# Gate biases joined to the modulation's sums, and gate and context rows moved ahead, in a two-block transformer kernel on one core

## The chip, the cores and the metric

The program runs on one core of a Trainium2 chip. Its time is the time of one execution on the device, in microseconds. Before the change three runs took 1168.17, 1168.83 and 1171.95 us; the median is 1168.83.

## What is computed

Everything is float32 with 256 tokens of width 1024. The first block (two layers of retention, dilated attention and a gated unit, each with a feed-forward) yields the latents `x`. The second block has one even and one odd layer, and a second set of 256 tokens, the context. The change lies in the second block:

```python
# mod, mod_ctx: silu(c) @ w_mod + b_mod, silu(c_ctx) @ w_mod + b_mod  -> shift, scale, gate of each layer
h_lat = rmsnorm(x, g) * (1 + scale) + shift            # the context with its own shift and scale
h_ctx = rmsnorm(ctx, g) * (1 + scale_c) + shift_c
y_l, y_c = even_layer(h_lat, h_ctx, ...)               # Fourier mixing and latent attention, @ w_out
x   = x + gate * y_l
ctx = ctx + gate_c * y_c                               # read only by the odd layer's norm
x   = x + gate_2 * odd_layer(norm(x), norm(ctx), ...)  # windowed attention over latents and context
```

So each layer has three vectors, shift, scale and gate, for the latents and three for the context; the odd layer needs no gate for the context.

## The kernel before

**Weights and precision.** All weights stream through SBUF. Each piece of 128 rows (`raw`) is cut into a high part (`whi`, written by ScalarE) and a low part (`wlo`, by VectorE or GpSimd), and each product is made of three on TensorE: high by high, high by low, low by high. Activations are cut in the same way into `xh` and `xl`, after transposes into a bank called `tr`; there are two such banks.

**Order of the work.** One Python class, `Flow` (L126), keeps an account of when each operand is expected. Weight products form the backbone, and the steps of everything else are tasks (generators) which `Flow` puts between them when their operands should be there. What it decides is only the order on each engine: an instruction whose operand is late holds all that stands behind it on its engine.

**Modulation.** `mod_step` (L871) multiplies pieces of `w_mod` with the two condition vectors and adds the sums in `macc`; the first sum of a group is copied there (L886 on). For a gate, group `g % 3 == 2`, the finished sums, still without bias, go to a DRAM tile `gates` as rows (`gates<-macc`). They must be read back on all 128 partitions.

**Gate rows.** `gate_rows` (L1659) reads half a gate row, 512 columns, to all partitions (`gr<-gates`, 256 KB), reads the same half of the bias (`brow<-in_b_mod`, 256 KB), both on ScalarE's DMA queue, and adds them on GpSimd (`gr<-gr,brow`).

**The even layer** runs as two passes whose steps are interleaved: pass 0 for the context, pass 1 for the latents. A pass ends with the output projection `wo`: for each half `h` of the columns it calls `gate_rows` (L2067), and for each tile `t` of 128 tokens it makes 24 products in a bank `mm`, multiplies by the gate on VectorE (`wt<-mm,gr`) and adds the old row. In pass 1 the sum goes into `x` (GpSimd). In pass 0 (L2087 on) the old half row is read from DRAM (`cr<-in_ctx`), the sum is made on GpSimd (`cr<-cr,wt`) and written to DRAM (`cnew<-cr`).

**The context's second norm.** After pass 0's `wo`, `ctx_task` (L2094) reads each whole row tile back (`junk<-cnew`, 512 KB) and starts `modnorm_task` (L1038) on it: a sum of squares on ScalarE (`dump`), its power -1/2 on VectorE and GpSimd (`pe`, `rmod`), the row times that on ScalarE (`junk<-junk,rmod`), eight transposes, scale and shift of each block on VectorE (`junk<-tr,modA,modT`), and the split (`xh`, `xl`). The same task serves the latents after pass 1's `wo`.

**Attention in pass 1** runs beside pass 0's `wo`: exponentials `pe` on ScalarE with their sums `den`, reciprocals `rd`, the scaled weights `pe<-pe,rd` (one half on VectorE, one on GpSimd), their transposes `tr<-c,pe`, and the split `pp`. Queries come as `qn`, `qp` and `qr`.

**The odd layer** loads its constants and, late, its gate `ogl`, again with `gate_rows` (L2300 on). `nsink` is a small constant row that VectorE negates.

Of the kernel before, what the change touches and what calls it, by code (L numbers as in the profile page):

```python
# [38 lines left out]
# column ranges of the packed constants  # L39
# [9 lines left out]
def make_constants():  # L49
# [10 lines left out]
    # the retention's decay, gamma ** (q - k), as a factor of each key and one of each query  # L60
# [6 lines left out]
    # dilated branches: how many of the three hold a key, as a bias on unscaled scores  # L67
# [29 lines left out]
def two_pi_parts():  # L97
    from fractions import Fraction
    # 1 / (2 pi), cut in pieces of 12 bits
# [12 lines left out]
class Ev:  # L112
    """Something a step waits for: the time at which its data is expected."""
# [6 lines left out]
LAT = 0.22          # from one engine's result to another's start  # L120
# [5 lines left out]
class Flow:  # L126
    """The order in which TensorE's work is issued: the weight products, with the steps of
    everything else put between them once their operands are expected to be ready.
    now: TensorE's time; chain: when the data of the step at hand is expected;
    lanes: when the other engines are expected to be busy."""  # L130
# [27 lines left out]
    # branches of a step that do not wait for one another  # L158
# [62 lines left out]
    def fill_gap(self, t):  # L221
        """Work that waits for nothing, where TensorE has none until t."""
        if self.spare is None or t - self.now < GAP:
            return False
        c = self.chain
        r = self.spare()
        self.chain = c
        return r
# [12 lines left out]
    def from_pe(self):  # L241
        """What follows reads the products issued last."""
        self.chain = self.now + LAT

# [15 lines left out]
class Lane:  # L260
    """An engine whose instructions are entered in the flow's account of time."""
# [34 lines left out]
class Slots:  # L296
# [22 lines left out]
    def give(self, slot):  # L319
        """Free once what the step at hand has issued is done."""  # L320
# [5 lines left out]
def block_kernel(ctx: ExitStack, tc: tile.TileContext, A, out, stop=None):  # L326
# [40 lines left out]
    # products, with what they are expected to take  # L367
# [17 lines left out]
    # the weights' rings: a part of each is block 1's alone  # L385
# [8 lines left out]
    # ------------------------------------------------------------------ constants  # L394
# [22 lines left out]
    # vectors that become columns: those of the first norm by themselves, for the start  # L417
# [29 lines left out]
    # ------------------------------------------------------------------ the stream of weights  # L447
# [17 lines left out]
    # how many pieces of w_mod are used at least after a chunk  # L465
# [4 lines left out]
    def ffn_order():  # L470
        """The chunks' products in the order in which they are issued, by rows of tokens."""
# [75 lines left out]
    spare = []        # places of the last pieces, besides the ring  # L547
# [4 lines left out]
    def load_ahead():  # L552
        """Loads in the order of the plan, as far as the rings go."""
# [18 lines left out]
    def load_mod():  # L572
        """The next pieces of w_mod, as far as their ring goes."""
# [9 lines left out]
    def pool_lo(key, i):  # L583
        """Whether a piece's low part is GpSimd's: DVE has much else."""
# [3 lines left out]
    def regroup(key, raw):  # L588
        """The columns of a piece as its parts shall have them: pairs of a range and its source."""
        if key[-1] in ("kvb", "qb"):  # L590
            # all heads' first 64 columns, then all heads' others
# [5 lines left out]
    def fill(upto=None, need=0):  # L597
        """Split as many pieces as the ring holds and are there; the first ones in any case."""
# [53 lines left out]
    def done(n=1):  # L652
        """The last uses of the next n pieces are issued."""
        del where[:n]
        fill()
# [8 lines left out]
    def mm3(o, xh, xl, w, first, last, c0=0, n=None):  # L664
        """Activations stationary."""
# [8 lines left out]
    def mmT(o, w, c0, xh, xl, first, last):  # L674
        """Weights stationary: 128 columns from c0."""
# [7 lines left out]
    # ------------------------------------------------------------------ split, transposed activations  # L683
    # four places of 128 tokens, in two pairs: XH[a][:, k, 128 b:128 b + 128], place 2 a + b
# [1677 lines left out]
```

## Time and profile before

| | before |
|---|---|
| median of 3 runs | 1168.83 us |
| lowest and highest run | 1168.17, 1171.95 us |
| span of the profiled execution | 1168.2 us; its own time is not listed apart, the lowest run took 1168.17 us |
| TensorE busy | 1080.1 us (92%), mean granted clock 0.971 |
| VectorE busy | 767.2 us (66%) |
| ScalarE busy | 610.7 us (52%) |
| GpSimd busy | 271.5 us (23%) |
| DMA | 189.84 MB, mean 163 GB/s |

TensorE is busy for nearly the whole span, so a wait elsewhere counts only where TensorE stands idle behind it, or runs at the lower clock after it. The profile's engine names are PE (TensorE), DVE (VectorE), ACT (ScalarE), POOL (GpSimd) and SP (the queue that loads weights); a `q` behind a name is the engine's instruction queue, which also issues DMAs. The last column of a timeline row is the idle time before it and what ended that.

### The profile page before, as it was taken

What the parts mean: (1) busy time and instruction counts of PE and PEld (TensorE: products, weight loads), DVE (VectorE), ACT (ScalarE), POOL (GpSimd) and SP (SyncE); (2) the same over time, 40 slices, a digit from 0 to 9 for tenths busy, and PEclk for the clock granted to TensorE, in tenths of its full rate; (3) what the DMA queues carried; (4) which work ended last, traced back from release to release, by engine and by line L of the source; (5) the groups of instructions that cost most, each with busy time, mean ns of one, the idle gap of its engine ahead of it and who ended that gap; (6) DMA issues with size and microseconds to landing.
All of it is one profiled execution on the core that took longest, in us unless ns stands there. A gap on an engine that the chain in (4) does not pass through costs nothing.

```text
span 1168.2 us, 17853 instructions
## 1 busy us (share of the span) xinstructions
PE 1080.1 (92%) x6602; PEld 936.2 (80%) x6602; DVE 767.2 (66%) x1410; ACT 610.7 (52%) x1176; POOL 271.5 (23%) x237
## 2 busy tenths in 40 slices
PE   6999999999999999989999997999879998999886
PEld 5899779989888888768999887789757886777765
DVE  6776675555547677657555546777756764688885
ACT  5564554434345644554444436776646653556653
POOL 4221100000001122100000014544563345354321
PEclk8999999999999999999999998999998999999998
DMA  8663677666755656468566624433454345343200
GB/s 262 211 194 122 197 217 253 182 219 215 238 162 165 211 164 207 136 222 282 183 190 187 200 81 135 143 86 107 159 173 142 93 151 161 90 132 121 73 1 37
DMA packets 117880, 189.84 MB, mean 163 GB/s; under 512 B 7043, under 2 KB 84208, under 8 KB 117792
## 3 DMA queue, kind: packets, MB, share of 16 engines
q1 hardware_dynamic: 112896, 179.33, 48.7%
q10 hardware_dynamic: 4528, 9.11, 2.5%
q8 instruction: 52, 0.85, 0.3%
q0 software_dynamic: 368, 0.25, 0.1%
q14 instruction: 36, 0.29, 0.1%
HBM read 186.55 MB, written 2.11 MB: 162 GB/s over the span
## 4 chain that ended last, share of the span: by engine, by line
PE 64%; DVE 13%; ACT 7%; issue 6%; DMA 5%; POOL 4%; ACTq 0%; DVEq 0%; POOLq 0%
PE mm L372 39%; PE sc L372 14%; PE tr L372 4%; PE tr L379 4%; PE s L372 3%; DVE wlo L280 3%; ACT whi L280 3%; DVE xl L280 2%; POOL wlo L280 1%; DMA cr<-in_ctx_dram 1%; DVE pp L280 1%; DMA brow<-in_b_mod_dram 1%; DMA raw<-in_w_in_dram 1%; DVE po L280 1%; DVE qn L280 1%
## 5 line engine op out<-in xcount | busy, mean ns | idle before, releaser
L280 DVE TENSOR_TENSOR wlo<-raw,whi 128x1024 fp32r<-128x1024 f32 (+3 forms) x260 | 316.5, 1222 | 170.4 <-ACT whi L280 165.6
L280 ACT ACTIVATE whi<-raw 128x1024 fp32r<-128x1024 f32 (+4 forms) x313 | 301.8, 973 | 228.1 <-PE mm L372 132.0
L372 PE MATMUL mm<-whi,xh 128*128 128x384 f32 (+2 forms) x564 | 219.9, 390 | 5.2 <-ACT whi L280 3.2
L372 PE MATMUL mm<-xh,whi 128*128 128x256 f32 x768 | 222.7, 290 | 0.3 <-DVE fh L280 0.3
L372 PE MATMUL mm<-xl,whi 128*128 128x256 f32 x768 | 216.8, 282 | 0.0
L372 PE MATMUL mm<-xh,wlo 128*128 128x256 f32 x768 | 216.7, 282 | 0.0
L372 PE MATMUL mm<-wlo,xh 128*128 128x384 f32 (+2 forms) x564 | 211.4, 375 | 5.1 <-DVE wlo L280 2.6
L372 PE MATMUL mm<-whi,xl 128*128 128x384 f32 (+2 forms) x564 | 210.6, 373 | 3.9 <-DVE xl L280 3.8
L280 POOL TENSOR_TENSOR wlo<-raw,whi 128x1024 fp32r<-128x1024 f32 (+4 forms) x53 | 112.9, 2132 | 242.8 <-ACT whi L280 232.9
L372 PEld LDWEIGHTS mm<-xh,whi 128*128 128x128 f32 x768 | 146.1, 190 | 4.3 <-issue 3.0
L372 PEld LDWEIGHTS mm<-xh,wlo 128*128 128x128 f32 x768 | 146.2, 190 | 1.2
L372 PEld LDWEIGHTS mm<-xl,whi 128*128 128x128 f32 x768 | 146.1, 190 | 0.0
L372 PEld LDWEIGHTS mm<-whi,xh 128*128 128x128 f32 x564 | 111.0, 197 | 21.5 <-ACT whi L280 4.3
L372 PEld LDWEIGHTS mm<-wlo,xh 128*128 128x128 f32 x564 | 110.9, 197 | 17.5 <-DVE wlo L280 3.9
L372 PEld LDWEIGHTS mm<-whi,xl 128*128 128x128 f32 x564 | 110.4, 196 | 17.4 <-DVE xl L280 5.1
L372 PE MATMUL sc<-whi,fhs 128*128 128x512 f32 x352 | 114.7, 397 | 0.0
L372 PEld LDWEIGHTS sc<-whi,fhs 128*128 128x128 f32 x352 | 66.2, 188 | 18.0 <-issue 2.1
L372 PE MATMUL sc<-wlo,fhs 128*128 128x512 f32 x176 | 69.8, 396 | 0.0
L280 POOL TENSOR_TENSOR rpost<-pe,mhalf 128x1 f32<-128x1 f32 x8 | 4.3, 542 | 257.6 <-DVE pe L280 257.6
L280 ACT ACTIVATE pp<-tr 128x512 fp32r<-128x512 f32 x56 | 33.0, 595 | 29.9 <-PE tr L379 27.6
L280 DVE TENSOR_TENSOR pp<-tr,pp 128x512 fp32r<-128x512 f32 x56 | 38.2, 685 | 14.1 <-ACT pp L280 13.8
L372 PE MATMUL tr<-rawm,mlh 128*32 128x256 f32 x384 | 41.0, 384 | 0.0
(350 smaller groups left out, 1621.9 us busy)
## 6 DMA issues: line engine op xcount, KB each, us to landing
raw<-in_w_gate_up_dram SPq DMA_DIRECT2D x72, 512.0 KB, 4.4
rawm<-in_w_mod_dram SPq DMA_DIRECT2D x48, 512.0 KB, 6.5
raw<-in_w_down_dram SPq DMA_DIRECT2D x44, 512.0 KB, 4.3
raw<-in_w_in_dram SPq DMA_DIRECT2D x56, 384.0 KB, 3.6
raw<-in_e_w_in_dram SPq DMA_DIRECT2D x24, 512.0 KB, 4.6
raw<-in_o_w_in_dram SPq DMA_DIRECT2D x20, 512.0 KB, 3.6
raw<-in_w_out_dram SPq DMA_DIRECT2D x16, 512.0 KB, 4.5
raw<-in_w_gate_up_dram SPq DMA_DIRECT2D x32, 256.0 KB, 4.8
```

The costliest lines, as they stand in the source:

```text
L280: return fn(*args, **kw)
L372: pe.matmul(o, lhsT, rhs, start=start, stop=stop_, **kw)
L379: pe.transpose(o, i, idt)
```

## The change

Five things change in the program.

1. The bias of the gates is loaded once at the start on the partitions where the gates' sums are made (`gbias`, four small DMAs on GpSimd's queue and a memset), and the first sum of a gate's group is not copied but added to it. `gates` in DRAM then holds the finished gate, and `gate_rows` is one DMA.
2. The even layer's gate rows are loaded by a task: for the context some time after the `kv` products, with the two row tiles of the context itself (`crow`, 512 KB each, which stay in SBUF); for the latents once pass 0's `wo` is issued.
3. The context's new rows are added into `crow` in place, and `modnorm_task` starts on them as soon as a tile's second half is added. The DRAM tile `cnew`, `cr` and `ctx_task` are gone.
4. The odd layer's gate row is loaded at the layer's start, right behind its constants.
5. The SBUF that is set aside for GpSimd's own DMA queue shrinks from its default to 4096 bytes per partition; `crow` and two `gr` are new tiles of the even layer.

```diff
+    gbias = b1p.tile([P, DEPTH, 256], F32, name="gbias")
+    gp.memset(gbias, 0.0)
+    def load_gbias():
+        for j in range(4):
+            o = 2 * D + 256 * j
+            gp.dma_start(gbias[32 * j:32 * j + 2], A["b_mod_2"][None, :, o:o + 256].to_broadcast([2, DEPTH, 256]))
...
-    cnew = dram.tile([2, P, D], F32, name="cnew")
...
-        if k == 0:
+        if k == 0 and g % 3 == 2:
+            dve.tensor_tensor(macc[:, mslot(g)], tr[:, :256], gbias[:, g // 3], op=OP.add)
+        elif k == 0:
             dve.tensor_copy(macc[:, mslot(g)], tr[:, :256])
...
             gp.dma_start(t_, cst[:, COL[name]:COL[name] + t_.shape[1]])
+        load_gbias()
...
     def gate_rows(dst, l, r, h):
         nc.scalar.dma_start(dst, gates[l, r:r + 1, h * 512:(h + 1) * 512].to_broadcast([P, 512]))
-        bm = work("brow")
-        o = 2 * D + h * 512
-        nc.scalar.dma_start(bm, A["b_mod_2"][l:l + 1, o:o + 512].to_broadcast([P, 512]))
-        gp.tensor_tensor(dst, dst, bm, op=OP.add)
...
+    rows_ev, wo_ev = [Ev(), Ev()], Ev()
+    crow = etile("crow", [2, D])
...
+        grs = []
+        def rows_task():
+            if b == 1:
+                yield wo_ev
+            else:
+                yield 10.0
+            for h in range(2):
+                grs.append(etile("gr", [512], 2))
+                gate_rows(grs[h], 0, 1 - b, h)
+            if b == 0:
+                for t in range(2):
+                    nc.scalar.dma_start(crow[:, t], cin[:, t])
+            F.set(rows_ev[b])
+        F.spawn(rows_task())
...
-            gr = work("gr")
-            gate_rows(gr, 0, 1 - b, h)
+            F.wait(rows_ev[b])
+            gr = grs[h]
...
-                    cr = work("cr")
-                    nc.scalar.dma_start(cr, cin[:, t, s])
-                    gp.tensor_tensor(cr, cr, tmp, op=OP.add)
-                    nc.scalar.dma_start(cnew[t, :, s], cr)
+                    gp.tensor_tensor(crow[:, t, s], crow[:, t, s], tmp, op=OP.add)
+                    if h == 1:
+                        F.spawn(modnorm_task(lambda t=t: crow[:, t], 1, 1, place(t), oev[0][t]))
         if b == 0:
-            def ctx_task():
-                yield 6.0
-                for t in range(2):
-                    cx = junk()
-                    nc.scalar.dma_start(cx, cnew[t])
-                    yield 3.0
-                    F.spawn(modnorm_task(lambda: cx, 1, 1, place(t), oev[0][t]))
-                    yield oev[0][t][1]
-            F.spawn(ctx_task())
+            F.set(wo_ev)
...
     dve.tensor_scalar(nsink, nsink, -1.0, None, op0=OP.mult)
+    gl = otile("ogl", [D])
+    for h in range(2):
+        gate_rows(gl[:, h * 512:(h + 1) * 512], 1, 0, h)
...
-    gl = otile("ogl", [D])
-    for h in range(2):
-        gate_rows(gl[:, h * 512:(h + 1) * 512], 1, 0, h)
...
-    nc = bacc.Bacc("TRN2", target_bir_lowering=False, num_devices=1)
+    nc = bacc.Bacc("TRN2", target_bir_lowering=False, num_devices=1, dynamic_dma_scratch_size=4096)
```

The rest of the diff drops comments. TensorE's order is the same up to about 800 us of the span and again from about 950 us on; between them tasks stand at other places.

ScalarE, in pass 0's `wo` where pass 1's first exponentials stand. Before:

```order
L2089 DMA cnew<-cr 128x512
L1664 DMA brow<-in_b_mod_dram 128x512
L280 ACTIVATE pe,den_8910<-s_8920,nb_8909 128x512
L280 ACTIVATE pe,den_8915<-s_8926,nb_8914 128x512
L280 ACTIVATE qn<-qT 64x256 x2
L280 ACTIVATE pe,den_8910<-s_8935,nb_8909 128x512
L280 ACTIVATE pe,den_8915<-s_8944,nb_8914 128x512
L2087 DMA cr<-in_ctx_dram 128x512
L280 ACTIVATE qn<-qT 64x256 x2
L280 ACTIVATE whi<-raw 128x1024 x2
L2089 DMA cnew<-cr 128x512
L280 ACTIVATE pp<-tr 128x512
```

The same place after the change:

```order
L1671 DMA gr<-gates 128x512
L280 ACTIVATE pe,den_8906<-s_8916,nb_8905 128x512
L280 ACTIVATE pe,den_8911<-s_8922,nb_8910 128x512
L280 ACTIVATE qn<-qT 64x256 x2
L280 ACTIVATE pe,den_8906<-s_8931,nb_8905 128x512
L280 ACTIVATE pe,den_8911<-s_8940,nb_8910 128x512
L280 ACTIVATE qn<-qT 64x256 x2
L280 ACTIVATE dump,ss<-crow 128x1024
L280 ACTIVATE whi<-raw 128x1024
L280 ACTIVATE crow<-crow,rmod 128x1024
L280 ACTIVATE pp<-tr 128x512
```

The DMAs of `cnew`, `brow` and `cr` are gone from it, and the context's sum of squares and its scaling by `rmod` now stand ahead of the first split `pp<-tr` behind the exponentials.

GpSimd at the same place. Before:

```order
L280 TENSOR_TENSOR wlo<-raw,whi 128x1024
L280 TENSOR_TENSOR qp<-qpe,qp 128x2x32 x4
L280 TENSOR_TENSOR gr<-gr,brow 128x512
L280 TENSOR_TENSOR pe<-pe,rd_8911 128x512
L280 TENSOR_TENSOR pe<-pe,rd_8916 128x512
L280 TENSOR_TENSOR cr<-cr,wt 128x512
L280 TENSOR_TENSOR wlo<-raw,whi 128x1024
L280 TENSOR_TENSOR qp<-qpe,qp 128x2x32 x4
```

After:

```order
L280 TENSOR_TENSOR qp<-qpe,qp 128x2x32 x4
L280 TENSOR_TENSOR crow<-crow,wt 128x512
L280 TENSOR_TENSOR wlo<-raw,whi 128x1024
L280 TENSOR_TENSOR crow<-crow,wt 128x512
L280 TENSOR_TENSOR pe<-pe,rd_8907 128x512
L280 TENSOR_TENSOR pe<-pe,rd_8912 128x512
L280 TENSOR_TENSOR rmod<-pe_9062,mhalf 128x1
L280 TENSOR_TENSOR wlo<-raw,whi 128x1024
```

The addition of the bias ahead of the two `pe` is gone and a context row's addition stands in its place; `rmod` comes behind them, ahead of a low part.

VectorE at the last transposed attention of pass 1 (`at`), just ahead of its `wo`. Before:

```order
L280 TENSOR_TENSOR at<-s_9778,avt 64x256
L280 SCALAR_TENSOR_TENSOR sgm<-sgm,mm 128x512
L280 TENSOR_TENSOR at<-at,sgm 128x512
L280 TENSOR_TENSOR xl_124<-at,xh_122 128x512 x2
L280 TENSOR_TENSOR wt<-mm,gr 128x512
```

After:

```order
L280 TENSOR_TENSOR at<-s_9768,avt 64x256
L280 SCALAR_TENSOR_TENSOR sgm<-sgm,mm 128x512
L280 TENSOR_TENSOR xl_124<-at,xh_122 128x512
L280 TENSOR_TENSOR at<-at,sgm 128x512
L280 TENSOR_TENSOR xl_124<-at,xh_122 128x512
L280 TENSOR_TENSOR wt<-mm,gr 128x512
```

The first of the two splits `xl` now stands ahead of the second `at`.

VectorE at the odd layer's start, with the latents' norm. Before, from the last `wt` on:

```order
L280 TENSOR_TENSOR wt<-mm,gr 128x512
L280 TENSOR_TENSOR wlo<-raw,whi 128x1024
L280 TENSOR_SCALAR junk<-tr,modA,modT 128x128 x6
L280 TENSOR_TENSOR xl_124<-junk,xh_122 128x4x128
L280 TENSOR_SCALAR junk<-tr,modA,modT 128x128 x2
L280 TENSOR_SCALAR pe_10147<-ss 128x1
L280 TENSOR_TENSOR xl_124<-junk,xh_122 128x4x128
L280 SCALAR_TENSOR_TENSOR ovs<-mm,ovs 128x4x64
```

After:

```order
L280 TENSOR_TENSOR wt<-mm,gr 128x512
L280 TENSOR_TENSOR wlo<-raw,whi 128x1024
L280 TENSOR_SCALAR junk<-tr,modA,modT 128x128 x8
L280 TENSOR_SCALAR nsink<-nsink 128x16
L280 TENSOR_TENSOR xl_124<-junk,xh_122 128x4x128 x2
L280 SCALAR_TENSOR_TENSOR ovs<-mm,ovs 128x4x64
L280 TENSOR_SCALAR pe_10130<-ss 128x1
```

The negation of `nsink`, which stood among the low parts ahead of this place, now stands between the eight scaled blocks and the latents' splits `xl`; on ScalarE the DMA of `nsink` is issued, with those of two constants ahead of it and the two `ogl` behind it, ahead of the `xh` of the same split.

## Rows read from the trace of the kernel before

**Rows 1.** Page, chain that ended last: share of the span by line.

```profile
PE mm L372 39%; PE sc L372 14%; PE tr L372 4%; PE tr L379 4%; PE s L372 3%; DVE wlo L280 3%; ACT whi L280 3%; DVE xl L280 2%; POOL wlo L280 1%; DMA cr<-in_ctx_dram 1%; DVE pp L280 1%; DMA brow<-in_b_mod_dram 1%; DMA raw<-in_w_in_dram 1%; DVE po L280 1%; DVE qn L280 1%
```

**Rows 2.** Stretches: busy PE, PEld, DVE, ACT, POOL (instructions), PEclk, DMA share, GB/s.

```profile
700.00:740.00 40.00, 33.19 (x201) 30.26 (x199) 29.98 (x58) 28.87 (x65) 17.75 (x15) 0.91 0.37 117
...
860.00:885.00 25.00, 15.95 (x67) 12.88 (x66) 15.19 (x18) 10.95 (x24) 13.87 (x16) 0.80 0.57 185
...
950.00:1000.00 50.00, 40.87 (x170) 32.85 (x169) 27.06 (x37) 19.63 (x28) 22.51 (x13) 0.90 0.52 159
```

**Rows 3.** Timeline, TensorE, 862 to 885: start us, us, engine, line, operation, count, [idle before].

```profile
864.60 0.39 PE L372 MATMUL mm<-whi,xl 128*128 128x512 f32 x1
...
869.34 1.19 PE L379 MATMUL tr<-c,pe 128*128 128x128 f32 x4 [4.36 <-POOL pe L280]
...
876.97 1.09 PE L379 MATMUL tr<-c,pe 128*128 128x128 f32 x4 [4.69 <-POOL qp L280]
...
879.99 0.63 PE L372 MATMUL mm<-whi,xh 128*128 128x512 f32 x1
```

**Rows 4.** Timeline, VectorE, 862 to 877.

```profile
862.90 0.52 DVE L280 TENSOR_TENSOR qn<-qT,qn 64x256 fp32r<-64x256 f32 x1 [1.31 <-ACT qn L280]
...
867.18 0.69 DVE L280 TENSOR_TENSOR wt<-mm,gr 128x512 f32<-128x512 f32 x1 [3.76 <-POOL gr L280]
...
871.06 3.90 DVE L280 TENSOR_TENSOR qn<-qT,qn 64x256 fp32r<-64x256 f32 x2
...
876.15 0.68 DVE L280 CAST qr<-tr 128x512 fp32r<-128x512 f32 x1
```

**Rows 5.** Timeline, GpSimd, 865 to 875.

```profile
865.88 1.26 POOL L280 TENSOR_TENSOR gr<-gr,brow 128x512 f32<-128x512 f32 x1 [2.00 <-DMA brow<-in_b_mod_dram]
...
868.02 1.27 POOL L280 TENSOR_TENSOR pe<-pe,rd 128x512 f32<-128x512 f32 x1 [0.88 <-DVE rd L280]
...
872.14 2.54 POOL L280 TENSOR_TENSOR wlo<-raw,whi 128x1024 fp32r<-128x1024 f32 x1
```

**Rows 6.** Tile brow: its DMAs from issue to landing.

```profile
DMA to landing us min/median/max: 3.4/5.5/7.6
```

**Rows 7.** Timeline, TensorE, 956 to 995.

```profile
956.90 0.50 PE L372 MATMUL mm<-whi,xl 128*128 128x512 f32 x1 [2.44 <-DVE xl L280]
...
981.63 1.97 PE L379 MATMUL tr<-c,junk 128*128 128x128 f32 x8 [3.50 <-ACT junk L280]
...
994.23 0.44 PE L379 MATMUL tr<-c,kn 128*128 128x128 f32 x2 [3.18 <-ACT kn L280]
```

**Rows 8.** Timeline, VectorE, 954 to 977.

```profile
954.01 4.53 DVE L280 TENSOR_TENSOR xl<-at,xh 128x512 fp32r<-128x512 f32 x2
...
976.35 0.69 DVE L280 TENSOR_TENSOR wt<-mm,gr 128x512 f32<-128x512 f32 x1 [7.32 <-POOL gr L280]
```

**Rows 9.** Timeline, GpSimd, 953 to 977.

```profile
953.49 2.81 POOL L280 TENSOR_TENSOR wlo<-raw,whi 128x1024 fp32r<-128x1024 f32 x1 [4.89 <-ACT whi L280]
...
956.26 1.73 POOL L280 TENSOR_TENSOR gr<-gr,brow 128x512 f32<-128x512 f32 x1
...
975.02 1.29 POOL L280 TENSOR_TENSOR gr<-gr,brow 128x512 f32<-128x512 f32 x1 [1.93 <-DMA brow<-in_b_mod_dram]
```

**Rows 10.** Timeline, ScalarE, 978 to 982.

```profile
978.43 1.06 ACT L280 ACTIVATE dump<-x 128x1024 bf16<-128x1024 f32 x1 [7.86 <-POOL x L280]
...
980.43 1.14 ACT L280 ACTIVATE junk<-x,rmod 128x1024 f32<-128x1024 f32 x1
```

**Rows 11.** Timeline, GpSimd, odd layer.

```profile
1053.56 2.50 POOL L280 TENSOR_TENSOR ogl<-ogl,brow 128x512 f32<-128x512 f32 x2
```

**Rows 12.** Chain of waits, 1040 to 1060: start us, us, what.

```profile
1045.14 4.83 DMA raw<-in_o_w_in_dram
```

**Rows 13.** Timeline, GpSimd, start of the program.

```profile
9.31 0.55 POOL L1092 DMA_DIRECT2D dil<-in_cst_dram  x1
```

**Rows 14.** Timeline, ScalarE, start of the program.

```profile
18.88 0.56 ACT L280 ACTIVATE v<-mm,rin 128x384 f32<-128x384 f32 x1
```

## What the change was predicted to do

> **What bounds the kernel now.** I read the page's chain first, to see whose time sets the end. It is TensorE's products, but two small transfers are named in it, the context's half rows `cr` and the bias rows `brow`, at 1% each of 1168 us [rows 1]. Next I read the busy time by stretches, to see where TensorE is short of work. Two stretches stand out: 860 to 885 us has 15.95 us of matmuls in 25 at a clock of 0.80, and 950 to 1000 has 40.87 in 50 at 0.90 [rows 2]. Only then the timelines of these two.
>
> In the first, TensorE ends a product at 864.99, then waits 4.36 us for `pe` and 4.69 more before the second transposes; after that a 512-column product takes 0.63 us where it took 0.39 [rows 3]. Those products start 0.43 us apart where they started 0.23 apart, which is the lower of the two clock levels (1.2 against 2.4 GHz). At full level the work from 864.99 to about 882.5 is some 4.2 us, so 13.3 us are lost: 9.05 to the two waits, about 4.25 to the clock. The chain behind it: VectorE's `wt` waits 3.76 us for GpSimd's `gr`, which itself waited for `brow` [rows 4, 5]. The reciprocals and `pe` stand behind this `wt`. The second wait is put down to `qp`, but what comes last is VectorE's `qr` at 876.15, which frees a transpose bank; two `qn` of 3.90 us stand ahead of it [rows 4].
>
> In the second stretch TensorE waits 2.44 us for `xl`, 3.50 for the scaled rows `junk`, 3.18 for `kn` [rows 7], 9.1 in all, with some 4 us more at the lower level behind them.
>
> **The start.** Four bias DMAs on GpSimd, at the 0.55 us of their neighbour at 9.31 [rows 13], make 2.2 us ahead of `rin`, whose first reader comes at 18.88 [rows 14]; before, the last of those DMAs ends at 9.86. The reader hides it unless GpSimd's DMA queue holds it. The second `rin` also moves behind a low part. Value +0.2 us, bounds 0 and +2.8 (a low part [rows 9] late by its whole length). The bias goes into `macc` by an addition in place of a copy, one VectorE instruction for one; more sums follow it before the gate goes out, so nothing.
>
> **Rows loaded ahead.** 1 MB of context rows and two gate halves go on ScalarE's queue at about 715 to 730 us, where the 16 DMA engines are busy 0.37 of the time [rows 2]. The weight stream's slack hides it; without it, the price is one late landing, 0 to +5.5 us (the median of `brow` [rows 6]). I take 0. Fourteen of the 22 row DMAs that ScalarE issued from 840 us on vanish.
>
> **First stretch.** `wt` can follow `qn`, which ends at 863.42, instead of starting at 867.18 [rows 4]: it ends at 864.1. GpSimd adds it into `crow` (1.28 us, priced as the `gr` addition) to 865.4 and does its `pe` by 866.6 (1.27 [rows 5]). TensorE is free at 864.99, so the first wait falls from 4.36 to 1.6. VectorE's second `pe` ends near 868.9, one `qn`, one power and a low part follow, `qr` is done near 871.4, and the second wait is about 2.5, not 4.69. ScalarE has a new wait: the first `pp` stands behind the scaling of `crow`, which waits for `rmod`, behind `crow`, `pe`, `pe` on GpSimd. `rmod` ends near 870.1 and the scaling (1.14 [rows 10]) near 871.3; behind it in ScalarE's queue are `pp`, low parts' sources and `qp`. In the old run `pp` was free to go at about 872.6, so this wait is just covered. The waits give 2.76 + 2.2 = 5.0. Of the clock's 4.25 I take 1.7 back, since shorter waits remain. Sum -6.7, bounds -3 (the first wait alone) and -10.
>
> **The context's norm, earlier.** Two tiles of `dump` (1.06), scaling (1.14), eight scaled blocks and splits come among pass 1's attention at 865 to 900 us, instead of 878 to 915. No instruction is new, they are denser. Value +1.5, bounds 0 and +5 (two `dump` and scaling pairs of 2.2 us held in full, 4.4, with some clock).
>
> **Second stretch.** (a) `xl`: the first of the two is issued ahead of `at`, at about 953.4, when its GpSimd neighbour starts, and `gr` (1.73) is gone behind that neighbour [rows 8, 9]. Of 2.44 and some 1.4 at the low clock I take -2.0, bounds 0 and -3.8. VectorE and GpSimd plainly hinder each other here: 4.53 us for two splits, of which one alone takes 0.69 elsewhere, ends right behind GpSimd's 2.81 and 1.73.
>
> The Trainium skill ("SBUF — State Buffer", section "Who interferes with whom") says that a VectorE instruction with two inputs in SBUF contends with a GpSimd instruction that reads SBUF, and that whichever was issued first decides who is blocked. The trace agrees, 4.53 us against twice 0.69. By that rule the 2.44 us belong to the low part of 2.81 us, not to `gr`, and (a) is 0 if GpSimd is still first; the sum would then be -10.3 instead of -12.3.
>
> (b) `junk`: `wt` of the first tile's second half waits 7.32 us for `gr` [rows 8], while its product is done at about 972.5. With `gr` there, `wt` ends at 973.2, `x` (1.29, as `gr` at 975.02 [rows 9]) at 974.5, `dump` and its read-out at 975.8, `rmod` near 976.6, the scaling at 977.8 [rows 10]; TensorE gets to the transposes at about 977.95, so 3.5 us go and with them about 1 of clock: -4.3, bounds -3 and -5. (c) `kn`: its product now ends near 984.5, `kn` can follow at 985.3, and TensorE wants it at about 987.2. That takes up to 3.18 and 1.4 of clock. Late next is `nsink`: its DMA is issued near 981, VectorE waits for it ahead of both `xl`. Landing takes 3.4 to 7.6 us as for `brow` [rows 6], so `xl` ends at 985.8 to 990, wanted at about 987.6. I take -3.0, bounds 0 and -4.6.
>
> **Odd layer.** Two additions of `ogl` (2.50 us [rows 11]) leave GpSimd ahead of a low part: -0.5, bounds 0 and -2.5. **Given back:** the weight stream is on the chain for 4.83 us in the odd layer [rows 12], and a kernel that arrives earlier may wait longer for it. I take half, +2.5, bounds 0 and +4.8.
>
> Sum: 0.2 - 6.7 + 1.5 - 2.0 - 4.3 - 3.0 - 0.5 + 2.5 = -12.3 us, made against the span of 1168.2; the median of the runs is 0.6 above it. So 1155.9 + 0.6 = 1156.5 us. With the terms' bounds taken as independent, about 6 us to each side: 1150 to 1162.5.
>
> **Rivals.**
> 1. The waits change owner: `qn` at 867 to 871 is again slowed by GpSimd (3.90 us for two, beside a low part of 2.54 [rows 4, 5]), so the second wait and the clock stay; `xl` too, and of `kn` only 1. Then 0.2 - 2.8 + 1.5 - 4.3 - 1 - 0.5 + 2.5 = -4.4: 1164.4, within 1162.5 to 1165.3. For it: both engines still do the same work there. Against: in the new order GpSimd's low part stands behind `rmod`, after `qn`.
> 2. The gain is given back: the rest of the odd layer is set by VectorE and by the arrival of weights, not by when it begins. Then the time is 1165.3 to 1172.3, say 1168. For it: the chain there holds a DMA of 4.83 [rows 12]. Against: the waits before 1000 us lie on TensorE, which hardly waits between 885 and 950.
> 3. Slower: the context's norm holds ScalarE ahead of `pp`. Its place is the first `pp` after the exponentials, its price, for one tile, `dump` and scaling 2.4 us and on GpSimd a row addition, two `pe` and a low part ahead of `rmod`, 1.3 + 2.3 + 2.5: 8.5, and the low clock once more, 4.25. It decides if `rmod` ends after about 871.5, so that `pp` goes later than the old 872.6. Then the first stretch's gain is gone: -12.3 + 6.7 - 1.5 + 8.5 + 4.25 = +5.6, 1174.4. For it: a ScalarE instruction that waits holds all `pp`. Against: `wt`, the head of that chain, is 3 us earlier.
> 4. All waits of both stretches and their clock vanish: about 21 us, 1147. For it: the row DMAs are the first cause of most. Against: `rmod`, `qr` and `nsink` remain.
>
> **Chances.** Forecast 0.56, rival 1 0.14, rival 2 0.12, rival 3 0.09, rival 4 0.09. A measurement of this kernel tells 0.3%, 3.5 us, from no change. Forecast, rivals 1 and 4 are faster by more: 0.79; rival 2 is within: 0.12; rival 3 slower: 0.09. The range leaves out rival 3, half of rivals 2 and 4's outer part: 1147 to 1168.5.
>
> **What would show it.** Right: no `gr` or `brow` among what `wt` waits for; first wait at the transposes of `pe` below 2 us, the second below 3; 860 to 885 us at a clock above 0.9; no wait on the latents' `junk` above 1 us. Wrong: `pp` waiting for the scaling of `crow`, `xl` waiting for `nsink`, TensorE waiting for weights where it did not, or a start later than before by over 1 us.

## The result, and the profile after

The changed kernel takes 1156.4 us (median of 4 runs, 1154.57 to 1158.27), against 1168.65 us (1168.17 to 1171.95) of the kernel before beside it. The ratio is 0.9883, with a 95% interval of 0.9858 to 0.9907: 12 us faster by the medians (13.7 by the ratio, which is not the quotient of the two medians), and within 0.1 us of the predicted 1156.5. One run of the kernel before, among the 17 beside the first four experiments, took 2071.76 us and is left out of the ratios. The terms of the sum came out less well than the sum. The profiled execution took 1157.96 us, 1.5 more than the median; its span is 1156.2, so 1.8 us lie around a span.

The chain of the page after answers to [rows 1]. It is followed back only to about 727 us, so its shares can't be set beside those of before; but it covers the stretch that matters, and `cr` and `brow` are not named in it.

```profile
PE mm L372 10%; PE s L372 4%; ACT whi L280 2%; PE tr L379 1%; POOL wlo L280 1%; DVE po L280 1%; DVE wlo L280 1%; PE tr L372 1%; DVE qn L280 1%; DVE pp L280 1%; DVE xl L280 1%; DMA raw<-in_o_w_in_dram 1%; DVE nb L280 1%; DVE junk L280 1%; DVE oat L280 1%
```

The stretches of after, with the columns of [rows 2]: busy PE, PEld, DVE, ACT, POOL (instructions), PEclk, DMA share, GB/s.

```profile
50.00:60.00 10.00, 8.80 (x52) 7.78 (x53) 8.35 (x16) 2.27 (x4) 4.93 (x5) 0.83 0.62 184
860.00:885.00 25.00, 22.18 (x111) 17.86 (x109) 16.14 (x27) 16.54 (x32) 14.53 (x13) 0.93 0.41 121
885.00:950.00 65.00, 58.59 (x402) 53.82 (x403) 47.62 (x82) 43.01 (x92) 23.16 (x18) 1.00 0.28 83
950.00:1000.00 50.00, 45.87 (x209) 36.46 (x208) 29.48 (x52) 24.79 (x40) 22.30 (x13) 1.00 0.43 136
```

Two stretches are better: 860 to 885 us has 22.18 us of matmuls instead of 15.95, at a clock of 0.93 instead of 0.80; 950 to 1000 has 45.87 instead of 40.87, at 1.00 instead of 0.90. One between them is worse: 58.59 us in 885 to 950, where before had

```profile
885.00:950.00 65.00, 62.41 (x420) 56.30 (x419) 46.73 (x82) 44.76 (x96) 27.82 (x21) 1.00 0.32 95
```

And 50 to 60 us, far ahead of the change's main part, ran at 0.83 in this execution; the same ten microseconds of before had 1.00.

TensorE after, from 862 to 985 us; the rows at 866.39, 870.82, 953.74, 972.51 and 981.20 answer to [rows 3, 7]:

```profile
866.39 0.83 PE L379 MATMUL tr<-c,pe 128*128 128x128 f32 x4 [0.17 <-POOL pe L280]
870.82 0.90 PE L379 MATMUL tr<-c,pe 128*128 128x128 f32 x4 [2.61 <-DVE qr L280]
...
875.45 0.60 PE L379 MATMUL tr<-c,pe 128*128 128x128 f32 x4
...
890.80 0.66 PE L379 MATMUL tr<-c,crow 128*128 128x128 f32 x4 [1.15 <-DVE crow L280]
896.11 0.63 PE L379 MATMUL tr<-c,crow 128*128 128x128 f32 x4 [2.56 <-DVE pp L280]
903.20 0.39 PE L372 MATMUL mm<-xh,wlo 128*128 128x256 f32 x1 [2.63 <-DVE wlo L280]
...
953.74 0.50 PE L372 MATMUL mm<-whi,xh 128*128 128x512 f32 x1 [2.09 <-ACT xh L280]
972.51 1.04 PE L379 MATMUL tr<-c,junk 128*128 128x128 f32 x8
981.20 0.44 PE L379 MATMUL tr<-c,kn 128*128 128x128 f32 x2 [0.80 <-ACT kn L280]
984.87 0.66 PE L379 MATMUL tr<-c,junk 128*128 128x128 f32 x4 [1.17 <-ACT junk L280]
```

In before the third of these transposes of `pe` stood at

```profile
882.51 0.60 PE L379 MATMUL tr<-c,pe 128*128 128x128 f32 x4
```

The wait of 4.36 us for `pe` is 0.17, that of 4.69 is 2.61, that for the `junk` of the latents' first tile is gone, that for `kn` fell from 3.18 to 0.80; a wait of 1.17 for the second tile's `junk` is new. New are three waits between 890 and 904, 6.3 us together, where before had 2.3 us in five waits of 0.28 to 0.58 from 893 to 924. Laying the two timelines side by side gives the ledger: after minus before at the same instruction is +2.3 us at 87 us, +2.1 at 838, -6.15 at the second transposes of `pe` (870.82 against 876.97), -7.1 at the third (875.45 against 882.51), -3.7 at the start of pass 1's `wo`, -13.0 at `kn` (981.20 against 994.23), -12.0 at the end.

The tile `gr`: what its readers and writers waited for, all of it. Before, `wt` waited three times for GpSimd's `gr`, 15.6 us together.

```profile
  PE mm L372: 7.3, 4
```

### The profile page after: what moved, and what is told of

It reads as the page before. It is cut to its first block, busy times and chain, and to the rows that moved or that the text cites. A ratio compares the mean times of both kernels' runs of the same rounds, so it can differ in the third digit from the quotient of the medians.

```text
span 1156.2 us, 17831 instructions
## 1 busy us (share of the span) xinstructions
PE 1073.7 (93%) x6602; PEld 932.0 (81%) x6602; DVE 760.9 (66%) x1410; ACT 610.9 (53%) x1176; POOL 265.6 (23%) x236
## 5 line engine op out<-in xcount | busy, mean ns | idle before, releaser
L280 POOL TENSOR_TENSOR wlo<-raw,whi 128x1024 fp32r<-128x1024 f32 (+4 forms) x53 | 110.4, 2085 | 250.1 <-ACT whi L280 245.8
```

The lines of the kernel that those rows point to most:

```text
L280: return fn(*args, **kw)
```

## The experiments

Times are medians; ratios are to runs of the kernel before on the same chip at the same time, with 95% intervals. The first five take the change apart. Every kernel here also carries item 5 of the change, the smaller space for GpSimd's DMA queue, which was not run by itself; the smallest gain below, 3.5 us, makes it unlikely that it is worth much.

**Biases joined, nothing else.** The kernel before, with `gbias` and the one-DMA `gate_rows` at their old places; the order on TensorE is that of before.

```diff
-        if k == 0:
+        if k == 0 and g % 3 == 2:
+            dve.tensor_tensor(macc[:, mslot(g)], tr[:, :256], gbias[:, g // 3], op=OP.add)
+        elif k == 0:
...
+        load_gbias()
...
-        nc.scalar.dma_start(bm, A["b_mod_2"][l:l + 1, o:o + 512].to_broadcast([P, 512]))
-        gp.tensor_tensor(dst, dst, bm, op=OP.add)
```

> Only the biases are joined to the modulation's sums; gate rows are still loaded at the wo loop and the context still goes through DRAM. Theory 1 (the waits were for brow and for GpSimd's addition, not for the gate row itself): gr is issued at its old place, 856.1 and 965.6, and lands 4.3 to 6.0 us later, ahead of the products that wt multiplies (863.4, 972.5), so both waits of wt go, and with them most of the stalls: 1155 to 1159 us, as fast as the full change. Theory 2 (the late issue of gr is what counts, so loading ahead is needed): wt waits for the landing of gr instead, and at most half of the gain comes: 1162 us or more.

1159.23 us (1158.35 to 1163.19), ratio 0.9914 [0.9895, 0.9933]: by the ratios 10 of the 13.7 us (0.0117 of 1168.65) come from this part alone. That is just above the 1155 to 1159 of theory 1 and rules out theory 2. On TensorE the first wait for `pe` is gone and the second is longer; two `qn` on VectorE take 3.90 us beside GpSimd. TensorE, VectorE and GpSimd of this kernel:

```profile
871.78 1.08 PE L379 MATMUL tr<-c,pe 128*128 128x128 f32 x4 [5.23 <-POOL qp L280]
...
865.87 3.90 DVE L280 TENSOR_TENSOR qn<-qT,qn 64x256 fp32r<-64x256 f32 x2
...
865.69 1.30 POOL L280 TENSOR_TENSOR cr<-cr,wt 128x512 f32<-128x512 f32 x1
866.96 2.52 POOL L280 TENSOR_TENSOR wlo<-raw,whi 128x1024 fp32r<-128x1024 f32 x1
```

This is rival 1's mechanism, waits that change owner: the second wait is 5.23 us here and 2.61 in the full change. The run without the context's part, below, has 3.21 there (at 869.95, for `qr`), so most of the difference goes without that part.

**Context on chip, nothing else.** The kernel before with `crow` loaded ahead, added in place and normed at once; gates still with `brow`.

```diff
+            for t in range(2):
+                nc.scalar.dma_start(crow[:, t], cin[:, t])
...
-                    gp.tensor_tensor(cr, cr, tmp, op=OP.add)
-                    nc.scalar.dma_start(cnew[t, :, s], cr)
+                    gp.tensor_tensor(crow[:, t, s], crow[:, t, s], tmp, op=OP.add)
+                    if h == 1:
+                        F.spawn(modnorm_task(lambda t=t: crow[:, t], 1, 1, place(t), oev[0][t]))
```

> Only the context's rows stay on chip, with its norm as early as in the full change; brow, its addition on GpSimd and the late gate rows are as before. Theory 1 (cr and cnew, 4% of the chain after 780 us, only stood behind gr): wt still waits for gr at about 867 and 976, the norm crowds pass 1's attention: 1166 to 1172 us, no gain. Theory 2 (the context's trips through DRAM are what the chain names them for): 1162 us or less.

1166.49 us (1163.05 to 1171.06, 12 runs), ratio 0.9970 [0.9954, 0.9986]: 3.5 us, a small gain within the time that theory 1 gave. The first stretch gained: its two waits are 2.33 and 2.26 us where before had 4.36 and 4.69, although `brow` is still there. The second stretch stays as it was:

```profile
865.16 0.66 PE L379 MATMUL tr<-c,pe 128*128 128x128 f32 x4 [2.33 <-POOL pe L280]
869.08 0.63 PE L379 MATMUL tr<-c,pe 128*128 128x128 f32 x4 [2.26 <-DVE qr L280]
...
977.85 1.09 PE L379 MATMUL tr<-c,junk 128*128 128x128 f32 x8 [3.40 <-ACT junk L280]
990.46 0.69 PE L379 MATMUL tr<-c,kn 128*128 128x128 f32 x2 [4.37 <-ACT kn L280]
```

**The whole change but for the context.** Gate rows loaded ahead, biases joined; `cr`, `cnew` and `ctx_task` as before.

```diff
-                    nc.scalar.dma_start(crow[:, t], cin[:, t])
...
-                    gp.tensor_tensor(crow[:, t, s], crow[:, t, s], tmp, op=OP.add)
...
+                    gp.tensor_tensor(cr, cr, tmp, op=OP.add)
+                    nc.scalar.dma_start(cnew[t, :, s], cr)
...
+            F.spawn(ctx_task())
```

> The full change without its context part: biases joined, gate rows loaded ahead, ogl early, but the context's new rows go through DRAM again and its norm starts late. Theory 1 (early norm costs the 1.15 + 2.56 + 2.63 us of waits at 890 to 903 us): 1151 to 1155 us, faster than the full change by 2 to 5. Theory 2 (the context part gives its share of the gain): 1158 to 1163.

1159.04 us (1157.88 to 1162.13), ratio 0.9909 [0.9891, 0.9926], the same as biases alone: loading the gate rows ahead adds nothing that these intervals could tell once a gate half is one DMA. The run is against my theory that the early context norm costs the new waits at 890 to 904 us. Here that norm is late again, the time is not shorter, and TensorE still waits 2.47 us behind `pp`:

```profile
896.13 0.54 PE L379 MATMUL tr<-identr,qp 128*128 128x128 f32 x4 [2.47 <-DVE pp L280]
...
892.67 2.80 DVE L280 TENSOR_TENSOR wlo<-raw,whi 128x1024 fp32r<-128x1024 f32 x1 [0.52 <-issue]
...
891.71 2.67 POOL L280 TENSOR_TENSOR wlo<-raw,whi 128x1024 fp32r<-128x1024 f32 x1 [2.58 <-ACT whi L280]
```

VectorE's low part, ahead of `pp`, takes 2.80 us beside GpSimd's; alone it takes 1.23. But this is not what stands ahead of `pp` in the full change. VectorE there, then GpSimd:

```profile
893.16 0.73 DVE L280 TENSOR_SCALAR crow<-tr,modA,modT 128x128 f32<-128x128 f32 x2
...
894.18 1.18 DVE L280 TENSOR_SCALAR pe<-pe,rd 128x512 f32<-128x512 f32 x1
895.29 0.68 DVE L280 TENSOR_TENSOR pp<-tr,pp 128x512 fp32r<-128x512 f32 x1
```

```profile
894.04 1.04 POOL L280 TENSOR_TENSOR pe<-pe,rd 128x512 f32<-128x512 f32 x1 [6.25 <-DVE rd L280]
```

The last four steps ahead of that `pp` are scaled blocks of the context's norm (`crow`), `rd` and `pe`; GpSimd was idle for 6.25 us before its `pe` and begins its next low part only at 896.35. So a wait of the same length has another path in each of the two kernels.

**Bias DMAs later.** The full change, with the four `gbias` DMAs behind the rope constants, at about 32 us instead of 10.

```diff
+        gp.tensor_scalar(gbias[:, 0, 0:128], rope[:, 0, :], 0.0, None, op0=OP.mult)
+        load_gbias()
...
-        load_gbias()
```

The first added line is there to make the DMAs wait for the rope constants.

> The full change with the four bias DMAs issued on GpSimd at about 31 us, behind the rotation tables, instead of ahead of rin (one small GpSimd instruction more); TensorE's order is that of the full change. Theory 1 (the 2.2 us by which the full change is late at 90 us comes from these DMAs and the shifted second rin): 2 us faster than the full change, 1153.5 to 1155. Theory 2 (it comes from when weights arrive, which varies by run): the same as the full change, 1156 to 1158.

1155.41 us (1153.04 to 1156.03), ratio 0.9868 [0.9848, 0.9887], not to be told from the full change. There was no lag at the start in this profile. But the profile of biases alone, with the DMAs at 10 us, had none either.

**Only the landing of the biases taken away.** The kernel before, with layer 0's two bias halves loaded once at about 710 us; GpSimd's addition stays.

```diff
+        if l == 0:
+            gp.tensor_tensor(dst, dst, brows[h], op=OP.add)
+            return
...
+                nc.scalar.dma_start(brows[h], A["b_mod_2"][0:1, o:o + 512].to_broadcast([P, 512]))
```

> The kernel before with one thing changed: layer 0's two bias halves are loaded once at about 715 us and kept, so that the late DMA of brow is gone, while GpSimd still adds the bias to each gate row at the old places (TensorE's order is that of before). Theory 1 (the landing of brow, 3.4 to 7.6 us behind other DMAs, is what wt waits for): most of the gain of joining the biases comes with it, 1158 to 1162 us. Theory 2 (GpSimd's addition and its place in GpSimd's queue is what wt waits for): 1165 us or more.

1163.47 us (1156.89 to 1164.78, 12 runs), ratio 0.9933 [0.9912, 0.9955]. It lies between the times of the two theories. By the ratios it gains 7.8 us where biases alone gained 10, with intervals that overlap: most is the landing; that the addition behind it in GpSimd's queue has the rest is likely, not shown. VectorE's `wt`, 3.76 us late in [rows 4], still waits 1.17, and in the second stretch 5.01 where [rows 8] has 7.32, there for an addition that stands behind a low part on GpSimd:

```profile
864.04 0.69 DVE L280 TENSOR_TENSOR wt<-mm,gr 128x512 f32<-128x512 f32 x1 [1.17 <-POOL gr L280]
...
967.77 0.69 DVE L280 TENSOR_TENSOR wt<-mm,gr 128x512 f32<-128x512 f32 x1 [5.01 <-POOL gr L280]
```

What is called landing here has two pieces. In before, the DMA of `brow` was issued well after that of `gr`, 4.5 us here and 3.5 in the second stretch (969.06 against 965.61):

```profile
856.09 0.44 ACTq L1661 DMA_DIRECT2D gr<-gates  x1
...
860.62 0.46 ACTq L1664 DMA_DIRECT2D brow<-in_b_mod_dram  x1
```

So the bias came late mostly because its DMA was issued late: in the first case behind the DMA of `cnew` in ScalarE's queue, in the second right at the end of a `wt`. What held it was not tested; `gr`, `brow`, `wt` and `cr` share three buffers (`work`), so a DMA may wait for an older tile's reader.

**The full change again**, twice, as the measure for its neighbours.

> The full change once more, on the same chip as the others of this group, for comparison. Theory 1 (start late by 2 us in some executions only): times spread over 1153 to 1159, ratio 0.986 to 0.990 of before.

1155.96 us (1153.09 to 1162.22), ratio 0.9882 [0.9847, 0.9917]. The profiled execution was the slowest, 1162.22. It had no lag at the start and the clock at 1.00 from 50 to 60 us, but 0.93 where the first profile had 1.00 in 1000 to 1100 us:

```profile
1000.00:1100.00 100.00, 93.22 (x506) 74.59 (x505) 81.30 (x168) 57.15 (x117) 41.10 (x24) 0.93 0.35 107
```

> The full change on the same chip as these two, for comparison: ratio 0.986 to 0.990 of before.

1156.02 us (1152.18 to 1159.74), ratio 0.9890 [0.9866, 0.9914].

**One low part off GpSimd, at `at`.** Full change; pass 1's `wo` low parts of the second half go to VectorE.

```diff
-        return i % a < b
+        return i % a < b and key != ("e", 1, "wo", 1)
```

> The full change with the low parts of the last output-projection weights of pass 1's second column half made by VectorE instead of GpSimd (two pieces; TensorE's order is that of the full change). Theory 1 (at is slowed from 0.67 to 2.86 us by GpSimd's low part of 2.70 beside it, and the 2.09 us wait of TensorE at xh comes from that): at takes 0.7 us, the wait falls below 0.7, and the kernel is 1 to 2 us faster than the full change, 0.1%. Theory 2 (at waits for something else): at stays at 2.9 us and the time does not fall.

1154.29 us (1151.68 to 1156.52), ratio 0.9862 [0.9831, 0.9893]. Within the interval of the full change, but the mechanism is plain. VectorE and GpSimd in the full change:

```profile
950.16 2.86 DVE L280 TENSOR_TENSOR at<-at,sgm 128x512 f32<-128x512 f32 x1
...
949.78 2.70 POOL L280 TENSOR_TENSOR wlo<-raw,whi 128x1024 fp32r<-128x1024 f32 x1 [4.90 <-ACT whi L280]
```

And in this run VectorE, then TensorE, whose wait falls from 2.09 to 0.34:

```profile
945.86 0.68 DVE L280 TENSOR_TENSOR at<-at,sgm 128x512 f32<-128x512 f32 x1
...
948.34 0.50 PE L372 MATMUL mm<-whi,xl 128*128 128x512 f32 x1 [0.34 <-DVE xl L280]
```

**The context's norm late.** Full change; the norm starts 12 us (by the planner's account) after `wo`, one tile after the other.

```diff
-                    if h == 1:
-                        F.spawn(modnorm_task(lambda t=t: crow[:, t], 1, 1, place(t), oev[0][t]))
...
+            def ctx_task():
+                yield 12.0
+                for t in range(2):
+                    F.spawn(modnorm_task(lambda t=t: crow[:, t], 1, 1, place(t), oev[0][t]))
+                    yield oev[0][t][1]
+            F.spawn(ctx_task())
```

> The full change with the context's norm started some 12 us after pass 0's output projection, one tile after the other, instead of at once for each tile; rows stay on chip. Theory 1 (the early norm costs the 6.3 us of waits at 890 to 903 us): 3 to 5 us faster than the full change. Theory 2 (the norm has to be somewhere and costs TensorE the same waits wherever it stands): within 1.5 us of the full change, or slower if it runs into pass 1's own end.

1159.2 us (1155.54 to 1162.62), ratio 0.9903 [0.9869, 0.9937]: not faster. The wait is 2.48 us again, at 896.79, behind a VectorE low part of 2.74 beside one of GpSimd's of 2.62. After the run without the context's part, this is the second sign that moving the norm away does not save this time. The path of the wait is that of the run without the context's part, not that of the full change.

```profile
896.79 0.53 PE L379 MATMUL tr<-identr,qp 128*128 128x128 f32 x4 [2.48 <-DVE pp L280]
```

**The other low part off GpSimd, at 896 us.** Full change; the one piece whose low part stands at 896.35 on GpSimd goes to VectorE.

```diff
-                    eng.tensor_tensor(lv, r, hv.bitcast(F32), op=OP.subtract)
+                    if i in (264,):
+                        F.op("pool", 0.06 + 2.0e-3 * 1024)
+                        nc.vector.tensor_tensor(lv, r, hv.bitcast(F32), op=OP.subtract)
+                    else:
+                        eng.tensor_tensor(lv, r, hv.bitcast(F32), op=OP.subtract)
```

> The full change with the low part of one piece of pass 1's Fourier gate weights made by VectorE instead of GpSimd (the one at 896.35 us; the order of all else is that of the full change). Theory 1 (the 2.6 us wait of TensorE at 903 us comes from GpSimd's low part, which slows VectorE's four qn from 1.7 to 3.8 us): qn takes 1.7 us, the wait at that place falls below 1 us, 1 to 2 us faster than the full change. Theory 2 (the context's norm has filled VectorE there): VectorE gets 1.2 us more, the wait stays at 2.6 us or grows, the time does not fall.

1154.35 us (1152.59 to 1156.96), ratio 0.9881 [0.9859, 0.9903]. Four `qn` in the full change, with GpSimd, and then in this run, with TensorE behind them:

```profile
896.20 3.83 DVE L280 TENSOR_TENSOR qn<-qT,qn 64x256 fp32r<-64x256 f32 x4
...
896.35 2.53 POOL L280 TENSOR_TENSOR wlo<-raw,whi 128x1024 fp32r<-128x1024 f32 x1 [1.27 <-ACT whi L280]
```

```profile
892.74 1.71 DVE L280 TENSOR_TENSOR qn<-qT,qn 64x256 fp32r<-64x256 f32 x4
...
897.61 0.38 PE L372 MATMUL mm<-xh,wlo 128*128 128x256 f32 x1 [0.50 <-DVE wlo L280]
```

The four take 1.71 us, and the wait that was 2.63 is 0.50. The other, 2.56 for `pp`, stays.

**Both low parts, and the bias DMAs late.** The three edits together.

> The full change with three edits together: bias DMAs behind the rotation tables, the last output-projection low parts on VectorE, and the one Fourier gate low part on VectorE. Theory 1 (GpSimd's low parts beside VectorE cost TensorE about 2 us at each of the two places): 1150 to 1153.5 us, ratio 0.982 to 0.986 of before. Theory 2 (these waits come back behind): as the full change, 0.987 to 0.989.

1151.56 us (1148.06 to 1154.4), ratio 0.9851 [0.9825, 0.9877]: 4.5 us below the full change on the same chip by the medians, though the intervals (0.9866 to 0.9914 there) still overlap. It is the fastest version of this study. Its profiled execution even began late: a DMA of positions, issued ahead of everything that the change touches, landed 1.5 us later than in before (GpSimd moved on at 9.54 instead of 7.99).

```profile
9.54 0.51 POOL L432 DMA_DIRECT2D junk<-in_e_kv_norm_dram  x1 [3.71 <-DMA posi<-in_positions_dram]
```

## Why the prediction was right, and where its terms were not

The mechanism held: `wt` waited for a gate row, the gate row for the bias's landing and GpSimd's addition, and reciprocals, `pe`, `x` and the norm stood behind that `wt`. Joining the biases alone gave 10 us. The parts add up, 10.1 and 3.5 against 13.7, as far as intervals of some 2 to 3 us to each side can tell. By the steps of the prediction, with lags of the two profiled executions:

- **The start**, +0.2 predicted, +2.3 in this execution. TensorE waited 2.63 us for `ropeq` at 51.20 instead of 1.74 at 50.44 and ran at 0.83 behind it. It isn't a fixed price of the bias DMAs: biases alone and the full change run again kept 1.00 there with the DMAs in place, and the fastest version showed 0.83 with them moved away. Over all profiles here the stretch has 0.83 in five of the eight with these DMAs at about 10 us and in one of the five without; whether they make it likelier stays open.
- **Rows loaded ahead**, 0, right as far as one execution shows: the lag was +2.3 us at 87 and +2.1 at 838, with those DMAs in between.
- **First stretch and the context's norm**, -6.7 + 1.5 = -5.2 predicted, -5.8 measured (+2.1 at 838 to -3.7 at 947), but made of other sizes. The two waits gave 6.27 (4.19 and 2.08; 5.0 predicted). The clock gave about 2.0, where I took 1.7: between the first and the third transposes of `pe` the lag fell by 4.1, 2.08 of it by the second wait. The granted clock of 860 to 885 us is 0.93, not 0.80, and products are at the full level (2.4 GHz) again at about 874 us instead of 882.5. Some 0.8 had been gained between 838 and the first wait, which no term had. From the third transposes (-7.1) to 947 (-3.7) 3.4 were lost.
- That loss I had put down to **the context's norm** (+1.5, with bounds to 5). Its size is inside the bounds; its cause is only in part the one I named. Of the three new waits, 2.63 us are VectorE slowed by GpSimd's low part: taking that away left 0.50. This is rival 1's mechanism, of which I had seen the place at 867 to 871 and not the one at 896. The other two, 1.15 and 2.56, stayed in that run. They stand before transposes of the context's norm itself, one for its scaled blocks and one for a `pp` behind such blocks, so they do fit the crowding that I named. But the norm can't be blamed for their whole length: the runs without the context's part and with the norm late have a wait of 2.47 and 2.48 us there by a low part, and are not faster. What the norm costs net stays open.
- **`pp` behind the scaling of `crow`**, the mechanism of the slower rival, came within 1 us of deciding. ScalarE after:

```profile
870.52 1.15 ACT L280 ACTIVATE crow<-crow,rmod 128x1024 f32<-128x1024 f32 x1 [3.23 <-POOL rmod L280]
871.57 0.58 ACT L280 ACTIVATE pp<-tr 128x512 fp32r<-128x512 f32 x1
```

  `rmod` ended near 870.5, where 871.5 was the point from which it would decide, and `pp` went at 871.57, right behind the scaling, but before the 872.6 of the old run.
- **`xl`**, -2.0 predicted; the wait only went from 2.44 to 2.09, and -1.7 was reached by the next `wt` (955.70 against 961.11, from a lag of -3.7 to -5.4) through the clock. The first `xl` went early as predicted, in 0.68 us; but `at`, now behind it, met GpSimd's low part and took 2.86. Two steps failed: the one that gave the delay to `gr` as well as to the low part (in before the wait ended at 956.90, 0.6 us after the low part and while the addition to `gr` still ran, to 957.99), and the one that did not ask what `at` would meet in the place that `xl` left. That the term came out near its value is luck. The Trainium skill ("SBUF — State Buffer", section "Who interferes with whom") had it right: GpSimd's low part was issued first, at 949.78, and VectorE's instruction with two inputs in SBUF waited for it. The prediction named this rule and took the other value.
- **`junk`**, -4.3 predicted: the first tile's wait of 3.50 is gone, and eight transposes take 1.04 us instead of 1.97, at full clock. **`kn`**, -3.0 predicted: 2.38 of 3.18 went. `nsink`, which I feared, waited for nothing. From pass 1's `wo` to `kn` the lag went from -3.7 to -13.0, 9.3 us, where the three terms made 9.3.
- **Odd layer and given back**, +2.0 together, measured +1.0 in this execution (-13.0 to -12.0); the weight stream took back little.
- **From span to time**: I set the median 0.6 above the span of before. Its profiled execution must have taken about 1170.0, an estimate from 1168.2 and the 1.8 that lie around a span in the runs on record, 1.3 above the median. The rule was wrong; the number survives, since the median lies below the profiled execution's own time in both kernels.
- **The signs.** Of those for being right, all came but one: TensorE waits 1.17 us for the second tile's `junk`, where the limit was 1. Of those for being wrong, two came and did not decide: `pp` did wait for the scaling of `crow`, and the start was later by more than 1 us.

The remaining errors are a start that was 2.1 us dearer in this execution, and stretches that were better by about as much. Agreement to 0.1 us is luck: three profiled executions of the full change have spans of 1155.6, 1156.2 and 1160.4 us. Agreement to a few us is not, since the waits that the forecast went by fell, save that of `xl`.

## What to carry to other kernels

A small transfer whose reader is an engine with other work behind it costs all that stands in that queue the time until it has been issued and has landed; add constants where a sum is made anyway, before the wide row exists. When a wait goes, look at which two instructions of VectorE and GpSimd now run side by side, since the collision can move to another place and take back part of the gain. Price a term by what TensorE waits for and by its clock behind the wait, and set it against several executions: here one profile differs from the next by more than most single terms.

## What was not expected of the hardware

VectorE beside GpSimd follows a sharp pattern in the profile of the full change. A VectorE `TENSOR_TENSOR` with both inputs in SBUF that starts while a wide one of GpSimd's runs does not slow down by a factor: it ends a fixed time after GpSimd's end, a little less than it takes alone. VectorE, then GpSimd, of the full change:

```profile
930.37 1.25 DVE L280 TENSOR_TENSOR wlo<-raw,whi 128x1024 fp32r<-128x1024 f32 x1
933.67 0.69 DVE L280 TENSOR_TENSOR pp<-tr,pp 128x512 fp32r<-128x512 f32 x1 [0.63 <-ACT pp L280]
...
960.93 2.17 DVE L280 TENSOR_TENSOR wlo<-raw,whi 128x1024 fp32r<-128x1024 f32 x1 [1.50 <-ACT whi L280]
973.86 2.58 DVE L280 TENSOR_TENSOR wlo<-raw,whi 128x1024 fp32r<-128x1024 f32 x1 [1.07 <-ACT whi L280]
```

```profile
929.25 1.28 POOL L280 TENSOR_TENSOR pe<-pe,rd 128x512 f32<-128x512 f32 x1 [6.78 <-PE mm L372]
933.53 2.40 POOL L280 TENSOR_TENSOR wlo<-raw,whi 128x1024 fp32r<-128x1024 f32 x1
...
959.61 2.41 POOL L280 TENSOR_TENSOR wlo<-raw,whi 128x1024 fp32r<-128x1024 f32 x1 [1.85 <-ACT whi L280]
972.95 2.40 POOL L280 TENSOR_TENSOR wlo<-raw,whi 128x1024 fp32r<-128x1024 f32 x1 [2.27 <-issue]
```

VectorE's low parts end 1.09, 1.08 and 1.09 us after GpSimd's instruction (931.62 against 930.53, 963.10 against 962.02, 976.44 against 975.35), whether GpSimd still had 0.16, 1.09 or 1.49 us to go. Alone such a low part takes 1.23. `at` of 128x512 ends 0.54 after it (953.02 against 952.48), alone it takes 0.68. `pp`, which has one input in PSUM, keeps its 0.69 us beside the same GpSimd low part. It is not only instructions with two inputs: the `TENSOR_SCALAR` `pe<-pe,rd`, with one tile as input, takes 0.49 us at 929.14, where it started ahead of GpSimd's, and 1.18 at 894.18 behind GpSimd's `pe` of 894.04, ending 0.28 after it. So what a collision costs is about what is left of GpSimd's instruction when VectorE's is issued, 2.2 us for `at` (2.86 instead of 0.68).

Executions of the same kernel differ by up to 11 us (1164.58 to 1175.63 for the kernel before on the chip of the second full-change run, 1153.09 to 1162.22 for the full change there), and in the profiles the mean granted clock of a stretch falls to 0.83 or 0.93, with a part of it at the lower level (1.2 GHz), in one place in one execution and in another in the next.
